# The last unit of a Hymba block: second token block in two halves, given queue orders, fewer sums between products, first block scaled by GpSimd

## The chip, the cores and the metric

The kernel runs on one core of one Trainium2 chip. The metric is device time in microseconds (us), as the median of several runs. TensorE (PE in the profile) multiplies matrices, VectorE (DVE) and ScalarE (ACT) work elementwise, GpSimd (POOL) too, but cannot read the accumulation banks (PSUM); SyncE (SP) issues the DMAs in this kernel. All engines run their own instructions in order and wait for each other through semaphores.

## The reference

One decoder layer on 2048 tokens of width 1024, in float32, cut to its outline:

```python
h = rmsnorm(x, norm1_g)
...                                   # projection, gated linear attention, short convolution
x = x + concatenate([o_gla, o_conv]) @ w_out
h2 = rmsnorm(x, norm2_g)
x = x + (silu(h2 @ w_ffn_gate) * (h2 @ w_ffn_up)) @ w_ffn_down     # 1024 -> 2816 -> 1024
return rmsnorm(x, norm_f_g)           # x * rsqrt(mean(x*x) + 1e-6) * norm_f_g
```

The change concerns the end of this: the last piece of the product with `w_ffn_down`, the residual addition, and the final rmsnorm of the last 1024 tokens.

## The kernel before

Data lie transposed: 128 partitions are 128 of the 1024 features, the free dimension is tokens. There are four blocks of 512 tokens (`PB`), handled as two halves of two blocks. A tile `y[d, j]` holds features 128d to 128d+127 (d from 0 to 7, `KD` = 8) of block j of the half.

Every operand of the big products is split in a high and a low fp32r part, by ACT (`act.activation(hi, src, AF.Copy)`, line 153) and VectorE (the difference, line 154). `product_step` then issues three matmuls per 128 features: high x high (line 381), high x low (382), low x high (383), each on 128x128 weights and 128x512 data. Most products go through `unit`, which computes a 2x2 block of outputs (two feature tiles r, two token blocks j) from seven instead of eight products; sums of weights for it run on GpSimd (lines 364 to 371).

The product with `w_ffn_down` is cut in four groups of inner features (`GROUPS`) and, within a group, in four units of two output tiles (d0 = 0, 2, 4, 6). In the last group of the second half each finished `y` is added up (line 982: on VectorE if the value lies in PSUM or r is not j, else on GpSimd), squared by ACT (lines 790 and 793) and added to `ssq[j]` by GpSimd (line 794), for the final norm.

The last unit of all (d0 = 6) is `last_unit`. It does without the seven-product scheme: four plain products, in the order (r, j) = (0,0), (1,0), (0,1), (1,1), each with 6 steps of 3 matmuls, 18 in all. `tc.issue_after` keeps this order on TensorE. After each product VectorE adds it to `y` (line 1059), ACT squares the result (line 1061), and ACT multiplies `y` by the norm's gain (`gain`, line 1028); the gains of the twelve earlier tiles are multiplied by ACT too, as those become ready. For a block's norm (`norm`) TensorE sums the squares over the partitions by two fp32 matmuls with a matrix of ones (lines 1033 and 1034), ACT takes Ln and Exp (lines 199 and 200), VectorE makes the mean (line 201) and one Newton step of three operations (lines 163 to 165), whose result `rb` lies in PSUM, and ACT copies it to SBUF (line 1036). `scale` then multiplies the eight tiles by `rb`: six on VectorE, two (d = 2 and 5) on GpSimd by the copy (line 1042), and SP stores each, 256 KB, to `out` (line 148).

Within these constraints a list scheduler, which follows a simulated timeline, orders each engine's instructions before the program runs; the order is then fixed. `bank()` takes one of 8 PSUM banks, `tt` and `bt` take SBUF tiles from shared rotating pools; where all are taken, the scheduler makes a new user wait for the release.

Of the kernel before, what the change touches and what calls it, by code (L numbers as in the profile page):

```python
# [14 lines left out]
ALU = mybir.AluOpType  # L15
# [36 lines left out]
def tile_hymba_block(ctx, tc, x, xt, win, wa, wgu, wout, wffn, wdown, wdown_first, small, out):  # L52
# [323 lines left out]
    def product_step(o, w, op, k, first):  # L376
        n = len(op)
        c = slice(k * P, (k + 1) * P)
        wh, wl = w[:, 0, c], w[:, 1, c]
        xh, xl = op[k][:, 0, :], op[k][:, 1, :]  # L380
        pe.matmul(o[:], wh, xh, start=first and k == 0, stop=False, skip_group_check=True)  # L381
        pe.matmul(o[:], wh, xl, start=False, stop=False, skip_group_check=True)  # L382
        return pe.matmul(o[:], wl, xh, start=False, stop=k == n - 1, skip_group_check=True)  # L383
# [634 lines left out]
    def last_unit(src, ops, b12, y, ssq):  # L1018
# [5 lines left out]
        with tc.issue_after(last_hi[0].ins):  # L1024
            act.preload_act_table_set("natural_log_exp_and_others")

        def gain(d, j):
            act.activation(y[d, j], y[d, j], AF.Copy, scale=col(C_GF + d))

        def norm(j, q):  # L1030

            tot, rb = bank("tot"), bank("rb")
            pe.matmul(tot[:], ones[:], ssq[j][:], start=True, stop=False)
            pe.matmul(tot[:], ones[:], q[:], start=False, stop=True)
            finish_rstd(ssq[j], tot, D, rb)
            act.activation(ssq[j][:], rb[:], AF.Copy)
            return rb

        def scale(j, rb):
            for d in range(KD):  # L1040
                eng, by = (pool, ssq[j]) if d in (2, 5) else (dve, rb)
                eng.tensor_tensor(y[d, j], y[d, j], by[:], ALU.mult)
                store(out[2 + j, :, d, :], y[d, j])

        for d in range(KD - 2):
            for j in range(2):
                gain(d, j)
        q, rbs = {}, []
        for j in range(2):
            for r in range(2):  # L1050
                o = bank()
                with ExitStack() as stack:
                    if j or r:
                        stack.enter_context(tc.issue_after(done.ins))
                    for i in range(2):
                        for k in range(len(b12)):
                            done = product_step(o, w[2 * r + i], columns[j][i], k, i == 0)
                yy = y[KD - 2 + r, j]
# [150 lines left out]
```

## Time and profile before

| | us |
|---|---|
| median of 3 runs | 2098.65 |
| the runs | 2098.31, 2098.65, 2102.15 |
| the profiled execution | 2102.39 |
| its span, first to last instruction | 2100.5 |
| mean granted TensorE clock | 0.992 |

The durations and start times in the prediction come from the profiled execution alone, counted from the start of its span. A row of the timeline reads: start, duration, engine, line, operation, output and inputs with their shapes, count; in brackets the idle time of the engine just ahead and the instruction that ended it. A row with a count above 1 merges neighbours. A row of the windows reads: the stretch, its length, busy time and count of PE, PEld (weight loads), DVE, ACT and POOL, then the granted clock of TensorE, the DMA engines' busy share, and GB/s. A row for one line of code reads: operations, minimum, median and maximum duration in ns, first and last start. SPq is SP's issuing of a DMA; the data move later. One fp32 matmul with the ones matrix appears as two records.

### The profile page before, as it was taken

To read this page: it belongs to the slowest core of one execution; us is meant where nothing else is said; L and a number is where in the kernel's file an instruction comes from. 1 tells how busy PE (TensorE), PEld (TensorE's weight loads), DVE (VectorE), ACT (ScalarE), POOL (GpSimd) and SP (SyncE) were. 2 spreads that over 40 slices of the span, in tenths; PEclk is the share of its full clock that TensorE was granted. 3 is DMA by queue.
4 is the path that set the end of the run, shared out by engine and by line. 5 is a ranking of instruction groups with operands and counts; after the bars stand their busy time and mean duration, and the time that the engine had idled before them with its cause. 6 is when DMAs were issued, how large, how long until landed. Compare 5 with 4: busy or idle time off the path is not lost.

```text
span 2100.5 us, 26873 instructions
## 1 busy us (share of the span) xinstructions
PE 2034.6 (97%) x9133; PEld 1649.8 (79%) x9133; DVE 1420.2 (68%) x1983; ACT 1003.2 (48%) x1990; POOL 971.9 (46%) x703
## 2 busy tenths in 40 slices
PE   6999999999999999999999999999999999999996
PEld 4768888877888878788888878787888888877774
DVE  7669786549743786788887665555767766665554
ACT  6555455656542345545545443333545444453344
POOL 3436322222102464465464338774655445436764
PEclk9999999999999999999999999999999999999998
DMA  7359495425686873655646687698444554587673
GB/s 279 129 167 318 128 340 158 149 81 167 205 281 236 325 251 105 236 200 214 223 175 220 236 314 269 234 344 321 159 178 165 192 210 174 213 340 271 259 270 110
DMA packets 189241, 464.43 MB, mean 221 GB/s; under 512 B 19824, under 2 KB 65072, under 8 KB 179504
## 3 DMA queue, kind: packets, MB, share of 16 engines
q1 hardware_dynamic: 189104, 462.72, 61.1%
q8 instruction: 72, 1.18, 0.2%
q14 instruction: 65, 0.53, 0.1%
HBM read 297.49 MB, written 165.15 MB: 220 GB/s over the span
## 4 chain that ended last, share of the span: by engine, by line
PE 74%; DVE 10%; DMA 8%; issue 3%; POOL 3%; ACT 3%; SPq 0%; DVEq 0%; POOLq 0%; ACTq 0%
PE mm L381 22%; PE mm L383 22%; PE mm L382 22%; DVE wq L154 2%; DVE h L508 2%; PE mm L812 1%; DVE op L154 1%; PE mm L813 1%; PE mm L815 1%; DVE so L154 1%; DMA raw<-in_wffn_dram 1%; DMA raw<-in_wdown_dram 1%; DMA op<-shT 1%; PE a_ps L576 1%; DVE c L405 1%
## 5 line engine op out<-in xcount | busy, mean ns | idle before, releaser
L381 PE MATMUL mm<-op,wq 128*128 128x512 f32 x2499 | 981.6, 395 | 17.8 <-ACT wq L153 7.4
L382 PE MATMUL mm<-op,wq 128*128 128x512 f32 x2499 | 976.9, 391 | 0.0
L383 PE MATMUL mm<-op,wq 128*128 128x512 f32 x2499 | 966.4, 392 | 10.4 <-DVE wq L154 9.6
L154 DVE TENSOR_TENSOR wq<-raw,wq 128x512 fp32r<-128x512 f32 (+2 forms) x626 | 527.7, 850 | 333.2 <-ACT wq L153 330.4
L153 ACT ACTIVATE wq<-raw 128x512 fp32r<-128x512 f32 (+2 forms) x626 | 363.5, 587 | 548.6 <-PE mm L383 391.5
L381 PEld LDWEIGHTS mm<-op,wq 128*128 128x128 f32 x2499 | 471.1, 189 | 132.0 <-ACT wq L153 13.5
L383 PEld LDWEIGHTS mm<-op,wq 128*128 128x128 f32 x2499 | 471.1, 189 | 121.2 <-DVE wq L154 22.6
L382 PEld LDWEIGHTS mm<-op,wq 128*128 128x128 f32 x2499 | 471.1, 189 | 97.0 <-issue 1.0
L366 POOL TENSOR_TENSOR raw<-s,raw 128x512 f32<-128x512 f32 (+2 forms) x97 | 127.6, 1316 | 422.6 <-DVE wq L154 402.5
L405 DVE TENSOR_TENSOR c<-mm,c 128x512 f32<-128x512 f32 x267 | 183.0, 685 | 94.4 <-PE mm L383 92.1
L364 POOL TENSOR_TENSOR s<-raw 128x512 f32<-128x512 f32 (+2 forms) x97 | 129.4, 1334 | 205.3 <-DMA raw<-in_wffn_dram 98.7
L371 POOL TENSOR_TENSOR raw<-raw 128x512 f32<-128x512 f32 (+2 forms) x97 | 126.8, 1307 | 129.6 <-DVE wq L154 122.4
L401 ACT ACTIVATE c<-mm 128x512 f32<-128x512 f32 x267 | 155.0, 586 | 39.0 <-PE mm L383 37.7
L794 POOL TENSOR_TENSOR ssx<-ssx,q 128x512 f32<-128x512 f32 x52 | 75.8, 1470 | 158.7 <-ACT q L793 158.5
L365 POOL TENSOR_TENSOR raw<-raw 128x512 f32<-128x512 f32 (+2 forms) x97 | 135.1, 1392 | 4.0
L982 POOL TENSOR_TENSOR y<-c,y 128x512 f32<-128x512 f32 x66 | 98.7, 1497 | 57.3 <-DVE c L405 53.2
L154 DVE TENSOR_TENSOR so<-t,so 128x512 fp32r<-128x512 f32 x100 | 90.7, 913 | 24.4 <-ACT so L153 24.0
L153 ACT ACTIVATE wq<-s 128x512 fp32r<-128x512 f32 (+2 forms) x97 | 56.8, 586 | 98.7 <-PE mm L383 86.0
L812 PE MATMUL mm<-op,wq 128*128 128x512 f32 x256 | 100.9, 395 | 0.0
L813 PE MATMUL mm<-op,wq 128*128 128x512 f32 x256 | 99.8, 390 | 0.0
L154 DVE TENSOR_TENSOR wq<-s,wq 128x512 fp32r<-128x512 f32 (+2 forms) x97 | 84.0, 866 | 17.0 <-ACT wq L153 16.4
L153 ACT ACTIVATE so<-t 128x512 fp32r<-128x512 f32 x100 | 62.5, 626 | 37.8 <-DMA sa_B<-so 16.1
(181 smaller groups left out, 1880.3 us busy)
## 6 DMA issues: line engine op xcount, KB each, us to landing
raw<-in_wffn_dram SPq DMA_DIRECT2D x44, 1024.0 KB, 6.1
sa_T<-so SPq DMA_DIRECT2D x88, 512.0 KB, 4.9
op<-sa_T SPq DMA_DIRECT2D x88, 512.0 KB, 9.4
sa_B<-so SPq DMA_DIRECT2D x69, 512.0 KB, 3.4
op<-sa_B SPq DMA_DIRECT2D x69, 512.0 KB, 9.0
raw<-in_win_dram SPq DMA_DIRECT2D x23, 1024.0 KB, 5.4
raw<-in_wdown_dram SPq DMA_DIRECT2D x24, 768.0 KB, 6.1
sx<-y SPq DMA_DIRECT2D x48, 256.0 KB, 3.3
```

The source lines that it names most:

```text
L153: last_hi[:] = [act.activation(hi, src, AF.Copy)]
L154: return dve.tensor_tensor(lo, src, hi.bitcast(F32), ALU.subtract)
L364: pool.tensor_tensor(s1, a21, a22, ALU.add)
L365: pool.tensor_tensor(a21, a11, a21, ALU.subtract)
L366: pool.tensor_tensor(a11, s1, a11, ALU.subtract)
L371: pool.tensor_tensor(a12, a12, a11, ALU.subtract)
L381: pe.matmul(o[:], wh, xh, start=first and k == 0, stop=False, skip_group_check=True)
L382: pe.matmul(o[:], wh, xl, start=False, stop=False, skip_group_check=True)
L383: return pe.matmul(o[:], wl, xh, start=False, stop=k == n - 1, skip_group_check=True)
L401: act.activation(t[:], o[:], AF.Copy)
L405: dve.tensor_tensor(t[:], o[:], t[:], ALU.add)
L812: pe.matmul(o[e, j][:], wh, m[:, 0, :], start=k == 0, stop=False)
```

## The change

Block 0 is still handled whole; block 1 is handled in two halves of 256 columns (tokens), `sa` and `sb`, through products, squares, sums, factor, scaling and stores. `queued` gives TensorE and VectorE one written-out order each for everything in the unit that goes through it. The sums use a matrix of 1/1024 (`means`) and Newton's step is rewritten, so that line 201's operation falls away and a constant -0.5 moves into the gains. Block 0's gains stay on ACT, for tiles 0 to 6; its tiles 0 to 6 are scaled by GpSimd, tile 7 by VectorE with gain and factor in one operation. All of block 1 is scaled by VectorE in that form, gain included; ACT multiplies no gains for block 1. The stores of block 1 are 16 of 128 KB instead of 8 of 256 KB.

```diff
@@ -373,14 +373,14 @@
         w["A22"] = weight_quarter(a22)
         return w
 
-    def product_step(o, w, op, k, first):
+    def product_step(o, w, op, k, first, s=slice(0, PB)):
         n = len(op)
         c = slice(k * P, (k + 1) * P)
         wh, wl = w[:, 0, c], w[:, 1, c]
-        xh, xl = op[k][:, 0, :], op[k][:, 1, :]
-        pe.matmul(o[:], wh, xh, start=first and k == 0, stop=False, skip_group_check=True)
-        pe.matmul(o[:], wh, xl, start=False, stop=False, skip_group_check=True)
-        return pe.matmul(o[:], wl, xh, start=False, stop=k == n - 1, skip_group_check=True)
+        xh, xl = op[k][:, 0, s], op[k][:, 1, s]
+        pe.matmul(o[:, s], wh, xh, start=first and k == 0, stop=False, skip_group_check=True)
+        pe.matmul(o[:, s], wh, xl, start=False, stop=False, skip_group_check=True)
+        return pe.matmul(o[:, s], wl, xh, start=False, stop=k == n - 1, skip_group_check=True)
 
     def unit(src, ops, into=None):
 
@@ -1023,50 +1023,124 @@
         columns = (ops["B11"], ops["B21"]), (b12, ops["B22"])
         with tc.issue_after(last_hi[0].ins):
             act.preload_act_table_set("natural_log_exp_and_others")
-
-        def gain(d, j):
-            act.activation(y[d, j], y[d, j], AF.Copy, scale=col(C_GF + d))
-
-        def norm(j, q):
-
-            tot, rb = bank("tot"), bank("rb")
-            pe.matmul(tot[:], ones[:], ssq[j][:], start=True, stop=False)
-            pe.matmul(tot[:], ones[:], q[:], start=False, stop=True)
-            finish_rstd(ssq[j], tot, D, rb)
-            act.activation(ssq[j][:], rb[:], AF.Copy)
+        known = bt("known", (P, P + KD))
+        means, gains = known[:, 0:P], known[:, P : P + KD]
+        dve.memset(means, 1.0 / D)
+        dve.tensor_scalar(gains, sml[:, C_GF : C_GF + KD], -0.5, None, ALU.mult)
+        halves = slice(0, PB // 2), slice(PB // 2, PB)
+        whole = slice(0, PB)
+        queues = {}
+
+        def queued(eng, issue):
+            with ExitStack() as stack:
+                if eng in queues:
+                    stack.enter_context(tc.issue_after(queues[eng].ins))
+                queues[eng] = issue()
+
+        def steps(o, r, j, s):
+            for i in range(2):
+                for k in range(len(b12)):
+                    queued(pe, lambda: product_step(o, w[2 * r + i], columns[j][i], k, i == 0, s))
+                    yield
+
+        def product(r, j, s):
+            o = bank()
+            for _ in steps(o, r, j, s):
+                pass
+            return o
+
+        def residual(o, r, j, s):
+            yy = y[KD - 2 + r, j][:, s]
+            queued(dve, lambda: dve.tensor_tensor(yy, o[:, s], yy, ALU.add))
+            q = tt("q")
+            act.activation(q[:, s], yy, AF.Square)
+            return q
+
+        def summed(tot, q, s, first=False, last=False):
+            queued(pe, lambda: pe.matmul(tot[:, s], means, q[:, s], start=first, stop=last))
+
+        def logs(j, tot, s):
+            l, y0 = bt("l"), bt("y0")
+            act.activation(l[:, s], tot[:, s], AF.Ln, bias=eps[:])
+            act.activation(y0[:, s], l[:, s], AF.Exp, scale=-0.5)
+            return l, y0
+
+        def factor(j, tot, s, l, y0):
+
+            rb = bank("rb")
+            queued(dve, lambda: dve.tensor_tensor(l[:, s], y0[:, s], y0[:, s], ALU.mult))
+            queued(
+                dve,
+                lambda: dve.scalar_tensor_tensor(
+                    l[:, s], tot[:, s], EPS, l[:, s], ALU.add, ALU.mult
+                ),
+            )
+            queued(
+                dve,
+                lambda: dve.scalar_tensor_tensor(
+                    rb[:, s], l[:, s], -3.0, y0[:, s], ALU.add, ALU.mult
+                ),
+            )
             return rb
 
-        def scale(j, rb):
-            for d in range(KD):
-                eng, by = (pool, ssq[j]) if d in (2, 5) else (dve, rb)
-                eng.tensor_tensor(y[d, j], y[d, j], by[:], ALU.mult)
-                store(out[2 + j, :, d, :], y[d, j])
+        def scale(ds, j, s, rb):
+            for d in ds:
+                yy, g = y[d, j][:, s], gains[:, d : d + 1]
+                queued(
+                    dve,
+                    lambda: dve.scalar_tensor_tensor(yy, yy, g, rb[:, s], ALU.mult, ALU.mult),
+                )
+                store(out[2 + j, :, d, s], yy)
+
+        def scale_beside(ds, j, s):
+            for d in ds:
+                yy = y[d, j][:, s]
+                pool.tensor_tensor(yy, yy, ssq[j][:, s], ALU.mult)
+                store(out[2 + j, :, d, s], yy)
 
         for d in range(KD - 2):
-            for j in range(2):
-                gain(d, j)
-        q, rbs = {}, []
-        for j in range(2):
-            for r in range(2):
-                o = bank()
-                with ExitStack() as stack:
-                    if j or r:
-                        stack.enter_context(tc.issue_after(done.ins))
-                    for i in range(2):
-                        for k in range(len(b12)):
-                            done = product_step(o, w[2 * r + i], columns[j][i], k, i == 0)
-                yy = y[KD - 2 + r, j]
-                dve.tensor_tensor(yy, o[:], yy, ALU.add)
-                q[j] = tt("q")
-                act.activation(q[j][:], yy, AF.Square)
-                gain(KD - 2 + r, j)
-                if not r:
-                    pool.tensor_tensor(ssq[j][:], ssq[j][:], q[j][:], ALU.add)
-                if j and not r:
-                    rbs.append(norm(0, q[0]))
-        rbs.append(norm(1, q[1]))
-        for j in range(2):
-            scale(j, rbs[j])
+            act.activation(y[d, 0], y[d, 0], AF.Copy, scale=gains[:, d : d + 1])
+
+        sa, sb = halves
+        tot = [bank("tot") for _ in range(3)]
+        o = product(0, 0, whole)
+        q = residual(o, 0, 0, whole)
+        act.activation(y[KD - 2, 0], y[KD - 2, 0], AF.Copy, scale=gains[:, KD - 2 : KD - 1])
+        pool.tensor_tensor(ssq[0][:], ssq[0][:], q[:], ALU.add)
+        o = product(1, 0, whole)
+        q7 = residual(o, 1, 0, whole)
+        o = product(0, 1, sa)
+        p = residual(o, 0, 1, sa)
+        pool.tensor_tensor(ssq[1][:, sa], ssq[1][:, sa], p[:, sa], ALU.add)
+        summed(tot[0], ssq[0], whole, first=True)
+        o = bank()
+        for n, _ in enumerate(steps(o, 1, 1, sa)):
+            if n == 2:
+                summed(tot[0], q7, whole, last=True)
+        l0 = logs(0, tot[0], whole)
+        p7 = residual(o, 1, 1, sa)
+        o = product(0, 1, sb)
+        summed(tot[1], ssq[1], sa, first=True)
+        rb0 = factor(0, tot[0], whole, *l0)
+        act.activation(ssq[0][:], rb0[:], AF.Copy)
+        scale_beside(range(KD - 1), 0, whole)
+        scale((KD - 1,), 0, whole, rb0)
+        r = residual(o, 0, 1, sb)
+        o = bank()
+        for n, _ in enumerate(steps(o, 1, 1, sb)):
+            if n == 0:
+                summed(tot[1], p7, sa, last=True)
+        l1 = logs(1, tot[1], sa)
+        summed(tot[2], ssq[1], sb, first=True)
+        summed(tot[2], r, sb)
+        rb1 = factor(1, tot[1], sa, *l1)
+        scale((0, 1), 1, sa, rb1)
+        r7 = residual(o, 1, 1, sb)
+        summed(tot[2], r7, sb, last=True)
+        l2 = logs(1, tot[2], sb)
+        scale((2, 3, 4, 5, 6, 7), 1, sa, rb1)
+        rb2 = factor(1, tot[2], sb, *l2)
+        scale(range(KD), 1, sb, rb2)
 
 
     act.preload_act_table_set("natural_log_exp_and_others")
```

## The prediction

> **What bounds the kernel now.** I read the share of the engines first, then the chain that ended last, then the timeline of the last 65 us engine by engine, then the windows of clock and DMA.
>
> ```profile
> PE 2034.6 (97%) x9133; PEld 1649.8 (79%) x9133; DVE 1420.2 (68%) x1983; ACT 1003.2 (48%) x1990; POOL 971.9 (46%) x703
> 2070.32 0.39 PE L381 MATMUL mm<-op,wq 128*128 128x512 f32 x1
> 2070.81 1.29 POOL L1064 TENSOR_TENSOR ssx<-ssx,q 128x512 f32<-128x512 f32 x1
> 2074.40 1.02 PE L1033 MATMUL tot<-ssx,ones 128*128 128x512 f32 x2
> 2075.26 1.02 PE L1034 MATMUL tot<-q,ones 128*128 128x512 f32 x2
> 2080.24 1.02 PE L1033 MATMUL tot<-ssx,ones 128*128 128x512 f32 x2
> 2080.80 3.68 DVE L1042 TENSOR_TENSOR y<-y,rb 128x512 f32<-128x512 f32 x6 [0.66 <-ACT ssx L1036]
> 2084.40 0.69 DVE L1059 TENSOR_TENSOR y<-mm,y 128x512 f32<-128x512 f32 x1
> 2085.80 2.07 PE L1034 MATMUL tot<-q,ones 128*128 128x512 f32 x2 [4.54 <-ACT q L1061]
> 2087.91 0.69 ACT L199 ACTIVATE l<-tot,eps 128x512 f32<-128x512 f32 x1 [1.41 <-PE tot L1034]
> 2088.63 0.63 ACT L200 ACTIVATE y<-l 128x512 f32<-128x512 f32 x1
> 2090.74 0.70 DVE L165 SCALAR_TENSOR_TENSOR rb<-l,y 128x512 f32<-128x512 f32 x1
> 2091.47 0.60 ACT L1036 ACTIVATE ssx<-rb 128x512 f32<-128x512 f32 x1 [2.22 <-DVE rb L165]
> 2092.10 3.68 DVE L1042 TENSOR_TENSOR y<-y,rb 128x512 f32<-128x512 f32 x6 [0.66 <-ACT ssx L1036]
> 2092.82 4.46 SPq L148 DMA_DIRECT2D out_dram<-y  x8
> 2093.50:2093.75 0.25, 0.00 (x0) 0.00 (x0) 0.25 (x1) 0.00 (x0) 0.25 (x1) 0.50 0.38 147
> 2098.00:2099.00 1.00, 0.00 (x0) 0.00 (x0) 0.00 (x0) 0.00 (x0) 0.00 (x0) 0.50 1.00 389
> 2099.20:2099.40 0.20, 0.00 (x0) 0.00 (x0) 0.00 (x0) 0.00 (x0) 0.00 (x0) 0.50 0.04 10
> ```
>
> TensorE is busy for 97% of the span, but the change lies behind its last products. Those end where the sums for block 1 begin, at 2080.24. From there to 2100.5 nothing is bound by products. The addition for the last product (L1059) starts only at 2084.40, because six scalings of block 0 hold VectorE from 2080.80: some 4 us. The sum behind it finds TensorE idle for 4.54 us and takes 2.07 us. Then come Ln, Exp, three VectorE steps, a copy, and scaling from 2092.10. All 2 MB of block 1 leave after that: the first bytes move at about 2093.65, 0.83 us behind their issue at 2092.82, and at 389 GB/s they last until 2099.2. The span ends 1.3 us later.
>
> **The products in halves.** The first product of block 1 starts at 2070.32 and its 18 matmuls take 4.08 us, 0.227 each. The change makes 36 such matmuls into 72 with 256 columns. No row shows that form; the nearest is the mixer's fp32 matmul, where a record loads 128 columns and streams 128 columns twice, 256 in all (the ones-matmul's two records for 512 columns take 0.86 us, four passes):
>
> ```profile
> 329.23 0.38 PE L736 MATMUL o_ps<-vt,scores 128*128 128x128 f32 x2
> 330.79 0.39 PE L738 MATMUL o_ps<-carry,kq 128*128 128x128 f32 x2
> L736 PEld LDWEIGHTS o_ps<-vt,scores x128: 187/192/192, 290.1 to 648.4; 128*128 128x128 f32 x128
> ```
>
> Fourteen records lie between these two starts: 0.111 each. The weight load's 0.19 us is thus overlapped, and I take 0.113, half of 0.227. The ends are 0.111 and the 0.227 of today. The sums: from 2074.40 to 2075.26 one ones-matmul takes 0.86, so half a one 0.43. TensorE's line from 2070.32: 18 halves (2.03), the first sum of block 0 (0.86), 9 halves (1.02), its second sum (0.86), to 2075.09; 9 and 18 halves, to 2078.14; half a sum, three halves, half a sum (1.20), to 2079.34; 15 halves, to 2081.04; two half sums, to 2081.9. The last product is issued 0.8 later than today's, since two whole and two half sums stand between the products where two whole ones did. One place is tight: GpSimd's addition to block 0's squares ends at 2072.1 (2070.81 + 1.29), and TensorE now asks for it at 2072.35; were it later, every half product would wait behind that sum.
>
> **VectorE and GpSimd.** The durations:
>
> ```profile
> L508 DVE SCALAR_TENSOR_TENSOR h<-h,sml,rb_ps x48: 732/736/749, 14.9 to 1068.5; 128x512 f32<-128x512 f32 x48
> L702 DVE SCALAR_TENSOR_TENSOR kq<-kq,ee x16: 410/425/1518, 212.8 to 627.1; 128x256 f32<-128x256 f32 x16
> L1042 POOL TENSOR_TENSOR y<-y,ssx 128x512 f32<-128x512 f32 x4 | 5.0, 1268 | 12.3 <-ACT ssx L1036 12.3
> 1206.38 0.42 DVE L154 TENSOR_TENSOR wq<-raw,wq 128x256 fp32r<-128x256 f32 x1
> 1207.58 2.98 DVE L154 TENSOR_TENSOR wq<-raw,wq 128x256 fp32r<-128x256 f32 x2 [0.18 <-ACT wq L153]
> 1207.54 1.30 POOL L915 TENSOR_TENSOR t<-c,t 128x512 f32<-128x512 f32 x1 [1.49 <-DVE c L911]
> 1208.80 1.48 POOL L915 TENSOR_TENSOR t<-c,c 128x512 f32<-128x512 f32 x1
> L699 ACT ACTIVATE ee<-ee 128x256 f32<-128x256 f32 x16 | 6.6, 413 | 18.4 <-DMA ee<-sd 16.9 <-DMA vt<-sv 1.5
> ```
>
> The new scaling is the form of L508 (data, a column of gains, a factor in PSUM), 0.736 whole. Half of it I take as 0.47, less 0.27 as between whole and half tensor_tensor (0.69 and 0.42), and 0.40 back to back, since six of today's take 3.68. Operations with both inputs in SBUF are another matter: L702 takes 0.41 or 1.52, and the pair at 1207.58, 0.42 each alone, takes 2.98 with GpSimd operations at 1207.54 and 1208.80: each waits for one of GpSimd's to end, and GpSimd's next is 0.18 longer. In the new factor the square of y0 and the last step read SBUF twice; the middle one reads PSUM.
>
> VectorE's line: Block 0's sum is readable at 2075.3, Ln and Exp (0.69, 0.63) end at 2076.65. The half addition for the (1,1) half, 2076.35 to 2076.77; factor of block 0, 3 x 0.70, to 2078.9. ACT copies the factor (0.60) and GpSimd starts seven multiplications at 2079.5, 1.27 each. One scaling (0.70), one half addition (0.42), to 2080.0. Block 1a's Ln and Exp (0.45 each, from L699's 0.41 for an activation) end at 2080.45. Its factor costs 3 x 0.38 = 1.14 alone; beside GpSimd I add half an operation's wait before the first step and what is left of the next after the middle step, 1.15 in all: to 2082.75. Two half scalings (0.84) and the last addition (0.42), to 2083.97: it starts 0.85 ahead of today's, and only half the width is left. Behind it queue six half scalings (2.4), to 2086.4. They hide the last square (0.42), half sum (0.43, 0.2 to drain), Ln and Exp, which end at 2085.9. Were that cover gone, its 1.9 would count. The second factor, beside GpSimd, 2.0, to 2088.4; eight half scalings, 3.2, to 2091.6. GpSimd ends at 2079.5 + 8.9 + four insertions of 0.33, about 2089.7; its last store isn't late.
>
> **Stores.** Sixteen stores become 24 on SP's one queue.
>
> ```profile
> 208.79 1.85 SPq L145 DMA_DIRECT2D vt<-sv  x4
> 210.69 1.85 SPq L145 DMA_DIRECT2D gt<-sg  x4
> ```
>
> Eight small ones start every 0.475 us (1.90 between groups of four); the eight of 256 KB above took 4.46, 0.56 each, at the rate the data moves (0.68). A 128 KB store needs 0.34 at 389 GB/s, so SP's issue is the limit. The last eight start at 2088.9, and I put two of GpSimd's among them (its sixth ends at 2088.1): nine gaps of 0.475, so the last issue is at 2093.2, past VectorE's 2091.6. Add 0.83 to first bytes, 0.34 to move, 1.3 to the end: 2095.7, against 2100.5: **4.8 less**. Rows of 1 KB instead of 2 have no row here; the data would have to fall to 276 GB/s (128 KB in 0.475) before they count. The bounds: SP keeps up with VectorE, 6.4 less; SP at 0.56, and so 1.0 behind from the twelve stores since 2083.2, 3.1 less. Half matmuls of 0.227 give 1.3 less (rival 2).
>
> Against the move to GpSimd speaks the page GPSIMD Engine Reference of the Trainium skill (Engine selection), which sends elementwise work with two inputs to VectorE, as about twice slower on GpSimd. The trace agrees on the ratio, 1.27 against the 0.69 of a whole tensor_tensor. Done by that rule, seven operations of 0.69 would stand in VectorE's line, which sets the end here, and the sum would be 4.8 worse; by the rows the line goes without them, and GpSimd's 10.2 fit beside it.
>
> **Ahead of the unit.** Today's gains run on ACT for both blocks; the change keeps block 0's alone, and seven of them. A memset and a column of gains are new on VectorE, small and early; it idles for 32% of the span.
>
> ```profile
> 2033.17 0.63 ACT L793 ACTIVATE q<-y 128x512 f32<-128x512 f32 x1 [1.78 <-DVE y L982]
> 2033.84 0.72 ACT L1028 ACTIVATE y<-y,sml 128x512 f32<-128x512 f32 x1
> 2034.47 0.92 ACT L153 ACTIVATE wq<-raw 128x384 fp32r<-128x384 f32 x2
> 2036.21 0.63 ACT L793 ACTIVATE q<-y 128x512 f32<-128x512 f32 x1 [0.83 <-DVE y L982]
> 2037.38 0.62 PE L381 MATMUL mm<-op,wq 128*128 128x512 f32 x1 [2.59 <-ACT c L401]
> 2038.66 0.63 PE L381 MATMUL mm<-op,wq 128*128 128x512 f32 x1
> 2039.94 0.63 PE L381 MATMUL mm<-op,wq 128*128 128x512 f32 x1
> 2049.73 1.32 ACT L1028 ACTIVATE y<-y,sml 128x512 f32<-128x512 f32 x2
> 2053.87 0.50 PE L381 MATMUL mm<-op,wq 128*128 128x512 f32 x1 [0.33 <-ACT c L401]
> ```
>
> The gain at 2033.84 follows the square of a DVE-added value of block 1 (row not equal to column in the unit) and stands ahead of a weight split; TensorE then idles 2.59 us, waiting for ACT, and runs nine matmuls at 0.43 (three in 1.28). The gain gone, 0.6 of the idle goes; the pair at 2049.73 likewise takes the 0.33 at 2053.87. I count 1.0 less. The bounds: 2.8 less, if the shorter idle keeps the clock up (nine times 0.2), and nothing; beyond nothing, a rival below.
>
> **Sum.** 4.8 + 1.0 = 5.8 less. The profiled execution took 2102.39, its span 2100.5 and 1.9 around it; it would take 2096.6. It lies 3.7 above the median of the runs, 2098.65, one of which took 2102.15; I take the difference off the median: 2092.9.
>
> **Rivals.** A measurement here can tell about 0.2%, 4.2 us, from no change.
>
> (1) *The lock and SP's queue eat it.* If each of the four double-SBUF steps waits for a whole GpSimd operation (L702: 1.52 instead of 0.43, 1.1 each, 4.4 where I count 2.1), or SP's stores wait in order behind GpSimd's, the tail saves 2.5 and the whole about 3.5: 2095.2, within 0.2%. For it, seven GpSimd operations back to back; against it, the pair at 1207.58, where VectorE got in between. The page SBUF — State Buffer of the Trainium skill (Who interferes with whom) says that the later one is blocked fully, which is this rival.
>
> (2) *Half-width matmuls that aren't half.* Slower: if 256 columns went at the pace of the fp32 ones-matmul, 0.43 each, the products would end at 2103.9 (2070.32, 72 x 0.43, 1.72 and 0.86 of sums); then addition, square and half sum with their drains 1.7, Ln and Exp 0.9, factor 1.14, the first scaling 0.47, seven store gaps 3.3 and 2.5 of tail, 10.0 in all: 2113.9, 13.4 more, a time of 2112.0. Decided by the pitch: at 0.227 the products end at 2089.2 and the span at 2099.2; slower begins above 0.24, and by 0.2% above 0.30. Against it, 0.111 at 329 to 331.
>
> (3) *ACT's order ahead of the unit.* With eight gains gone the instructions are interleaved anew, and a copy may stand behind a later square as at 2036.21. One new stall of the size at 2037.38 costs 2.6 + 1.8 = 4.4: 2097.3, no change; two of them, 2101.7.
>
> (4) *The order isn't kept:* if the last addition still followed all of block 1a's scalings, 2.4 would return: 2095.3; it is put into VectorE's order, so I give it nothing.
>
> **How the numbers follow.** Forecast 0.68, 2089.5 to 2094.4 (both best bounds at the low end); rival 1: 0.15; rival 2: 0.07, of which 0.06 slower; rival 3: 0.10, of which 0.06 slower. So faster 0.68, same 0.15 + 0.01 + 0.04 = 0.20, slower 0.12. The range, 2089.5 to 2098.9, takes in rival 1 and one stall of rival 3 and leaves out the slower cases and a little at the low end.
>
> **What would show it.** Right: matmuls of 128x256 starting every 0.11 to 0.12; the last addition at about 2084 less what is saved ahead; GpSimd busy for about 10 us without a gap; SP's last eight stores every 0.48; TensorE's idle at 2037 shorter. Wrong: a pitch near 0.2; the factor's steps at 1.5 each; TensorE idling ahead of 2066 where it doesn't now; the last store over 3 us behind the last scaling.

## The result and the profile after

| | us |
|---|---|
| before, median of 22 runs | 2102.96 |
| after, median of 22 runs | 2098.03 |
| ratio after / before | 0.9974, 95% interval 0.9967 to 0.998 |
| the profiled execution after | 2099.24 |
| its span | 2097.2 |
| mean granted TensorE clock | 0.993 |

The change makes the kernel faster by 0.26%, 4.9 us between the medians (5.5 by the ratio, 4.2 to 6.9 by its interval). Both medians lie higher than the 2098.65 that was shown before; the ratio, taken side by side, is what counts.

Single executions of this kernel drift against each other by several microseconds long before the last unit. Therefore I read the end of every trace from a mark of its own: the start of the first matmul of block 1 in `last_unit`. From it to the end of the span I call the *tail*: 30.18 us before (2100.5 less 2070.32) and 25.56 after (2097.2 less 2071.64), 4.62 less.

The shares of the engines on the page after:

```profile
PE 2034.3 (97%) x9175; PEld 1652.7 (79%) x9175; DVE 1415.2 (67%) x1993; ACT 997.8 (48%) x1984; POOL 975.4 (47%) x706
```

Nothing is to be learnt there: TensorE's 97% hides a change of 4.6 us. The timeline of the end, after, engine by engine:

```profile
2071.64 0.28 PE L381 MATMUL mm<-op,wq 128*128 128x256 f32 x1
2073.67 0.28 PE L383 MATMUL mm<-op,wq 128*128 128x256 f32 x1
2082.81 0.59 PE L1060 MATMUL tot<-ssx,known 128*128 128x256 f32 x2
2085.85 0.70 PE L1060 MATMUL tot<-q,known 128*128 128x256 f32 x2 [2.01 <-ACT q L1056]
2082.18 0.49 DVE L1071 TENSOR_TENSOR l<-y 128x256 f32<-128x256 f32 x1
2083.16 0.94 DVE L1080 SCALAR_TENSOR_TENSOR rb<-l,y 128x256 f32<-128x256 f32 x1
2084.93 0.42 DVE L1054 TENSOR_TENSOR y<-mm,y 128x256 f32<-128x256 f32 x1
2085.26 2.43 DVE L1091 SCALAR_TENSOR_TENSOR y<-y,known,rb 128x256 f32<-128x256 f32 x6
2087.61 0.42 DVE L1071 TENSOR_TENSOR l<-y 128x256 f32<-128x256 f32 x1
2088.52 0.92 DVE L1080 SCALAR_TENSOR_TENSOR rb<-l,y 128x256 f32<-128x256 f32 x1
2089.47 3.22 DVE L1091 SCALAR_TENSOR_TENSOR y<-y,known,rb 128x256 f32<-128x256 f32 x8
2081.10 9.46 POOL L1098 TENSOR_TENSOR y<-y,ssx 128x512 f32<-128x512 f32 x7 [5.42 <-ACT ssx L1125]
2081.83 13.05 SPq L148 DMA_DIRECT2D out_dram<-y  x24
2092.02 1.89 SPq L148 DMA_DIRECT2D out_dram<-y  x4
2094.00 0.88 SPq L148 DMA_DIRECT2D out_dram<-y  x2
```

The last addition (L1054, 2084.93) no longer stands behind block 0's scalings: counted from the mark it starts at 13.3 instead of 14.1, with half the width left, and the six scalings behind it cover the last square, sum, Ln and Exp: VectorE stands idle for no longer than 0.04 at a time between 2081.06 and 2092.69. The last scaling ends 21.05 after the mark instead of 25.46, 4.41 less; the stores, now 24, end 4.62 less. What the data did, in the windows of the same trace (the last number of a row is GB/s):

```profile
2083.00:2084.00 1.00, 0.84 (x4) 0.38 (x3) 0.97 (x2) 0.00 (x0) 1.00 (x2) 1.00 1.02 385
2088.00:2089.00 1.00, 0.00 (x0) 0.00 (x0) 0.93 (x3) 0.00 (x0) 1.00 (x1) 0.50 1.00 362
2094.00:2095.00 1.00, 0.00 (x0) 0.00 (x0) 0.00 (x0) 0.00 (x0) 0.00 (x0) 0.50 0.78 265
```

With 256 KB stores alone the DMA engines are full at 385. At 2088 they are full at 362, with 128 KB stores (rows of 1 KB) of block 1 and 256 KB stores of GpSimd's tiles side by side; what the small ones reach alone is seen in e4. At the very end they are not full: 265 GB/s is one 128 KB store every 0.49 us, the pace at which SP issues them (four from 2092.02 to 2094.00).

### The profile page after: what moved, and what is told of

It is laid out like the page before. It is cut to its first block, busy times and chain, and to the rows that moved or that the text cites. A ratio compares the mean times of both kernels' runs of the same rounds, so it can differ in the third digit from the quotient of the medians.

```text
span 2097.2 us, 26987 instructions
## 1 busy us (share of the span) xinstructions
PE 2034.3 (97%) x9175; PEld 1652.7 (79%) x9175; DVE 1415.2 (67%) x1993; ACT 997.8 (48%) x1984; POOL 975.4 (47%) x706
## 4 chain that ended last, share of the span: by engine, by line
PE 76%; DVE 9%; DMA 7%; issue 3%; POOL 2%; ACT 2%; SPq 0%; DVEq 0%; ACTq 0%; POOLq 0%
PE mm L381 23%; PE mm L383 23%; PE mm L382 22%; DVE wq L154 2%; DVE h L508 2%; PE mm L812 1%; PE mm L813 1%; PE mm L815 1%; DVE so L154 1%; DVE op L154 1%; DMA raw<-in_wdown_dram 1%; DMA op<-shT 1%; DMA raw<-in_wffn_dram 1%; PE a_ps L576 1%; DVE c L405 1%
## 5 line engine op out<-in xcount | busy, mean ns | idle before, releaser
L154 DVE TENSOR_TENSOR wq<-raw,wq 128x512 fp32r<-128x512 f32 (+2 forms) x626 | 525.0, 846 | 334.2 <-ACT wq L153 332.1
L401 ACT ACTIVATE c<-mm 128x512 f32<-128x512 f32 x267 | 155.0, 586 | 38.7 <-PE mm L383 37.5
L794 POOL TENSOR_TENSOR ssx<-ssx,q 128x512 f32<-128x512 f32 x52 | 75.8, 1469 | 158.7 <-ACT q L793 158.5
L982 POOL TENSOR_TENSOR y<-c,y 128x512 f32<-128x512 f32 x66 | 99.0, 1502 | 58.0 <-DVE c L405 58.0
L154 DVE TENSOR_TENSOR so<-t,so 128x512 fp32r<-128x512 f32 x100 | 90.2, 906 | 24.9 <-ACT so L153 24.6
L154 DVE TENSOR_TENSOR wq<-s,wq 128x512 fp32r<-128x512 f32 (+2 forms) x97 | 83.9, 865 | 17.0 <-ACT wq L153 16.5
```

Source lines behind the costliest of these rows:

```text
L154: return dve.tensor_tensor(lo, src, hi.bitcast(F32), ALU.subtract)
L401: act.activation(t[:], o[:], AF.Copy)
```

## The experiments

The theory (A): nearly all of the gain comes from one thing, that VectorE adds the last product before it scales block 0, not after. Its rivals: it needs the halves (B), or it needs GpSimd's share of the scalings (C). For what is left behind it the end may be set by SP's issue (S), by the data rate (D), or by VectorE's line (V). Into this line counts what I call the lock: a VectorE step with two inputs in SBUF waits while a GpSimd operation runs; e5 tests it. In the table, all times but the ratio are from the profiled execution; the end of the last scaling and the tail are counted from the mark.

| kernel | mark | span | last scaling ends | tail | tail less before | ratio to before, 95% interval |
|---|---|---|---|---|---|---|
| before | 2070.32 | 2100.5 | 25.46 | 30.18 | | |
| after | 2071.64 | 2097.2 | 21.05 | 25.56 | -4.62 | 0.9974 (0.9967 to 0.998) |
| e1, before with the order alone | 2067.57 | 2093.7 | 21.39 | 26.13 | -4.05 | 0.9979 (0.9969 to 0.999) |
| e2, after without halves | 2074.99 | 2102.7 | 22.88 | 27.71 | -2.47 | 0.9986 (0.9975 to 0.9997) |
| e3, after, VectorE scales block 0 | 2074.25 | 2101.2 | 23.61 | 26.95 | -3.23 | 0.9981 (0.9968 to 0.9994) |
| e4, after, two issuing queues | 2069.28 | 2094.4 | 21.04 | 25.12 | -5.06 | 0.9973 (0.9963 to 0.9983) |
| e5, after without the lock | 2064.48 | 2089.4 | 19.78 | 24.92 | -5.26 | 0.9970 (0.9957 to 0.9983) |
| e6, after, early sums | 2073.20 | 2101.4 | 21.22 | 28.20 | -1.98 | 0.9987 (0.9975 to 0.9998) |
| e7, e4 + e5 + early sums | 2072.61 | 2096.9 | 19.81 | 24.29 | -5.89 | 0.9967 (0.9955 to 0.9979) |
| e8, before with the gains moved | 2067.74 | 2097.7 | 26.81 | 29.96 | -0.22 | one run |
| e9, e6 with the stores sorted | 2068.29 | 2093.5 | 21.21 | 25.21 | -4.97 | 0.9973 (0.9964 to 0.9983) |
| e10, e4 + e5 | 2066.68 | 2091.1 | 19.78 | 24.42 | -5.76 | 0.9973 (0.9962 to 0.9983) |

The ratios of the variants overlap; only against before do they stand alone. The comparisons among variants therefore rest on the tails, each from one execution. Of the computing in them, pairs in which it is the same show how well it repeats: the last scaling ends at 21.22 and 21.21 in e6 and e9, at 19.78 in e5 and in e10. How well the stores behind it repeat was not measured.

**e1: the order alone.** The kernel before, with one wait: block 0's scalings come after the last addition.

```diff
-                eng.tensor_tensor(y[d, j], y[d, j], by[:], ALU.mult)
+                with tc.issue_after(added.ins):
+                    eng.tensor_tensor(y[d, j], y[d, j], by[:], ALU.mult)
...
-                dve.tensor_tensor(yy, o[:], yy, ALU.add)
+                added = dve.tensor_tensor(yy, o[:], yy, ALU.add)
```

> The kernel before, with one thing of the change: the last product's addition stands ahead of block 0's six scalings in VectorE's order. The measure in the trace is the tail, from the first matmul of block 1's first product to the end of the span: 30.18 us before (2070.32 to 2100.5), 25.56 after (2071.64 to 2097.2). Theory A (most of the change's gain is that the last addition no longer waits for the scalings): addition at 2080.4 to 2081.1, square to 2081.8, sum on a warm TensorE to 2082.9, Ln and Exp to 2084.2; the six scalings fill VectorE to 2084.8, factor to 2087.6, copy wait 0.7, first store 0.7 later at 2089.0 instead of 2092.8: tail 26.3, 3.8 shorter, about 0.18% of the time. Rival B (the halves make the gain): the six scalings then stand ahead of the second factor instead and the 2 MB still leave at once: tail 29 or more.

The timeline of e1, and a row of its windows:

```profile
2077.69 0.69 DVE L1060 TENSOR_TENSOR y<-mm,y 128x512 f32<-128x512 f32 x1 [0.31 <-PE mm L383]
2078.29 3.67 DVE L1043 TENSOR_TENSOR y<-y,rb 128x512 f32<-128x512 f32 x6
2079.09 1.12 PE L1034 MATMUL tot<-q,ones 128*128 128x512 f32 x2 [0.59 <-ACT q L1062]
2085.28 3.68 DVE L1043 TENSOR_TENSOR y<-y,rb 128x512 f32<-128x512 f32 x6 [0.66 <-ACT ssx L1036]
2090.00:2091.00 1.00, 0.00 (x0) 0.00 (x0) 0.00 (x0) 0.00 (x0) 0.00 (x0) 0.50 1.03 385
```

VectorE waits 0.31 us for the last product and adds it; the six scalings start 0.24 later than before, counted from the mark (10.72 against 10.48), because before they had to wait 0.66 for ScalarE's copy anyway. In return the sum's idle time falls from 4.54 to 0.59 and the sum itself from 2.07 to 1.12. The tail is 4.05 shorter, 26.13 where A expected 26.3: one line of order gives most of what the whole change gives. Its end is set by data at 385 GB/s in full-size stores (the windows row).

**e2: the change without halves.** Block 1 goes whole through products, sums, factor and scaling; the order, GpSimd's seven scalings and the gains in the scaling stay. Both sums of block 0 stand right behind block 1's first product.

```diff
-        o = product(0, 1, sa)
-        p = residual(o, 0, 1, sa)
+        o = product(0, 1, whole)
+        p = residual(o, 0, 1, whole)
...
-        scale((2, 3, 4, 5, 6, 7), 1, sa, rb1)
-        rb2 = factor(1, tot[2], sb, *l2)
-        scale(range(KD), 1, sb, rb2)
+        scale(range(KD), 1, whole, rb1)
```

> The changed kernel with block 1 in one piece of 512 columns: given orders, GpSimd's seven scalings and the folded gains stay; both sums of block 0 come right behind block 1's first product. Theory A: the order and GpSimd carry the gain; last addition at about 2080.5 (on the time axis of before), factor beside GpSimd to 2087.5, eight scalings of 0.67, stores from 2088.2 at the data's 0.68 each with two of GpSimd's among them: tail 26.9, 3.3 shorter than before and 1.3 longer than after. Rival B (halves carry it): tail 29 or more.

Timeline and windows of e2:

```profile
2085.93 0.69 DVE L1054 TENSOR_TENSOR y<-mm,y 128x512 f32<-128x512 f32 x1
2089.87 0.93 DVE L1071 TENSOR_TENSOR l<-y 128x512 f32<-128x512 f32 x1 [3.26 <-ACT y L1065]
2085.31 9.52 POOL L1098 TENSOR_TENSOR y<-y,ssx 128x512 f32<-128x512 f32 x7 [3.31 <-ACT ssx L1119]
2090.00:2091.00 1.00, 0.00 (x0) 0.00 (x0) 0.96 (x2) 0.00 (x0) 1.00 (x2) 1.00 0.57 219
2098.00:2099.00 1.00, 0.00 (x0) 0.00 (x0) 0.00 (x0) 0.00 (x0) 0.00 (x0) 0.50 1.00 379
```

27.71, between the two expectations and 1.6 worse than the order alone. GpSimd yields one 256 KB tile in 1.36 us (9.52 over seven), 193 GB/s, and in the meantime VectorE has nothing to scale: it idles 3.26 us for the square, the sum, Ln and Exp. So the DMA engines run at 219 while they could do 380, and the rest is stored afterwards at 379. Without the halves, moving block 0 to GpSimd costs; that is read from these rows, since e2 and e1 also differ in the factor's steps and in the gains.

**e3: VectorE scales block 0.** The change with six of block 0's tiles on VectorE and two on GpSimd, as before.

```diff
-        scale_beside(range(KD - 1), 0, whole)
-        scale((KD - 1,), 0, whole, rb0)
+        scale_beside((2, 5), 0, whole)
+        scale((0, 1, 3, 4, 6, 7), 0, whole, rb0)
```

> The changed kernel with block 0 scaled as before the change: tiles 2 and 5 on GpSimd, six on VectorE, these with the gain folded in. Theory A (the end is set by the stores: in the trace after, the last one is issued 1.8 us behind VectorE's last scaling): VectorE's line grows by five whole scalings, 3.3, and loses up to 1.0 of waiting for GpSimd, so its end moves by 2.3 and the stores' by about 0.6 only: tail 26.2. Rival C (GpSimd's scaling is what gains): the whole 3.3 shows: tail 28.9.

The timeline of e3, with two rows of TensorE, and two rows of its windows:

```profile
2088.54 0.70 PE L1060 MATMUL tot<-q,known 128*128 128x256 f32 x2 [2.52 <-ACT q L1056]
2091.03 1.22 PE L1060 MATMUL tot<-q,known 128*128 128x256 f32 x2 [1.80 <-ACT q L1056]
2083.66 4.04 DVE L1091 SCALAR_TENSOR_TENSOR y<-y,known,rb 128x512 f32<-128x512 f32 x6 [0.72 <-ACT ssx L1124]
2088.86 0.43 DVE L1080 SCALAR_TENSOR_TENSOR rb<-l,y 128x256 f32<-128x256 f32 x1
2090.12 0.42 DVE L1054 TENSOR_TENSOR y<-mm,y 128x256 f32<-128x256 f32 x1
2094.64 3.22 DVE L1091 SCALAR_TENSOR_TENSOR y<-y,known,rb 128x256 f32<-128x256 f32 x8
2088.50:2089.50 1.00, 0.70 (x2) 0.30 (x2) 0.93 (x3) 0.00 (x0) 0.00 (x0) 1.00 1.03 383
2090.50:2091.50 1.00, 0.47 (x1) 0.47 (x2) 1.00 (x4) 0.42 (x1) 0.00 (x0) 0.52 0.94 339
```

26.95, nearer to A's 26.2 than to C's 28.9. The factor's last step is 0.43 beside an idle GpSimd instead of 0.94, but the six scalings stand ahead of the second half's additions again: the last addition starts 15.87 after the mark (2090.12) instead of 13.29, and the last scaling ends 2.56 later than after. Only 1.39 of it reaches the end, because the stores have less to catch up: the tail behind the last scaling falls from 4.51 to 3.34. The halves without GpSimd are, in this order, worth less than the order alone on whole blocks (-3.23 against -4.05). But e3 takes away GpSimd's share and the early place of the last addition at once: halves with block 0's scalings on VectorE behind the last addition were not tried. What is shown is that halves and GpSimd together give 0.57 over e1, and neither of them as e2 and e3 have it does.

**e4: a second issuing queue.** Every other store of the last half is issued by ScalarE, which has nothing else to do by then.

```diff
-                store(out[2 + j, :, d, s], yy)
+                if other and d % 2:
+                    act.dma_start(out[2 + j, :, d, s], yy)
+                else:
+                    store(out[2 + j, :, d, s], yy)
```

> The changed kernel with every other store of the last half issued by ACT, which is idle by then; nothing else differs. Theory S (SP's issue, 0.475 to 0.5 a store, sets the end): VectorE's last scaling sets it instead, and the end comes about 1.8 earlier: tail 23.8. Rival D (the data set it: the DMA engines are at 0.95 to 1.0 from 2087 to 2092.5, and 1.15 MB are left at 2092.0, 3.1 us at 366 GB/s): 0.7 earlier: tail 24.9.

Timeline and windows of e4:

```profile
2088.01 2.69 ACTq L1094 DMA_DIRECT2D out_dram<-y  x4
2091.00:2092.00 1.00, 0.00 (x0) 0.00 (x0) 0.00 (x0) 0.00 (x0) 0.00 (x0) 0.50 0.98 337
```

25.12: D's 24.9 is nearly met, S's 23.8 is not. The issue limit is gone (337 GB/s at a DMA share of 0.98 instead of 265 at 0.78), yet only 0.44 us of the tail goes with it: the data had a backlog, and in 128 KB stores alone, as in this row, the DMA engines are as good as full at 337, not at 385. The Trainium skill, DMA: Bandwidth & Descriptors (Issuing engines are not separate DMA queues), says that a second issuing engine saves the issue time alone, since the same 16 DMA engines do the work. The run agrees; that the issue time is usually small beside the transfer doesn't hold for this store, 0.49 against 0.39 (128 KB at 337 GB/s).

**e5: no lock.** Exp writes its result in the factor's PSUM bank and ScalarE squares it, so no VectorE step of the factor reads SBUF twice, and VectorE has two steps instead of three.

```diff
-            l, y0 = bt("l"), bt("y0")
+            l, y0 = bt("l"), bank("rb")
...
+            act.activation(l[:, s], y0[:, s], AF.Square)
...
-            rb = bank("rb")
-            queued(dve, lambda: dve.tensor_tensor(l[:, s], y0[:, s], y0[:, s], ALU.mult))
+            rb = y0
```

> The changed kernel with the factor rebuilt so that no step of it has two inputs in SBUF: Exp is written to the factor's own PSUM bank, ACT squares it (one more ACT operation a factor), and VectorE has two steps instead of three. Tail after: 25.56 (first matmul of block 1's first product to the end of the span). The factors of the two halves take 1.92 and 1.83 there, with the last step at 0.93. Expected: last steps at 0.43 to 0.47, VectorE's last scaling 1.0 earlier. Theory D (since e4: the data of the stores set the end, near full rate from five us behind the first store): the tail shortens by 0.4 at most, to 25.2. Rival V (VectorE's line sets the end): all of the 1.0 shows, 24.6.

The timeline of e5:

```profile
2080.12 0.42 DVE L1074 SCALAR_TENSOR_TENSOR l<-tot,l 128x256 f32<-128x256 f32 x1 [0.24 <-ACT l L1066]
2080.58 0.43 DVE L1080 SCALAR_TENSOR_TENSOR rb<-l,rb 128x256 f32<-128x256 f32 x1
2073.79 8.68 POOL L1098 TENSOR_TENSOR y<-y,ssx 128x512 f32<-128x512 f32 x7 [5.28 <-ACT ssx L1125]
```

24.92, in the middle between D (25.2) and V (24.6). The last step falls from 0.92 to 0.43, and GpSimd's operation from 1.35 to 1.24 in the mean: the lock cost both sides. The last scaling ends 1.27 earlier, not by the lock alone, since e5 also takes a VectorE step out of each factor. Of this, 0.64 arrives at the end; the rest waits behind the data and SP.

**e6: earlier sums.** Both sums of block 0 right behind the first half product, and its factor ahead of the addition of the second.

```diff
-        for n, _ in enumerate(steps(o, 1, 1, sa)):
-            if n == 2:
-                summed(tot[0], q7, whole, last=True)
+        summed(tot[0], q7, whole, last=True)
         l0 = logs(0, tot[0], whole)
...
+        o = product(1, 1, sa)
+        p7 = residual(o, 1, 1, sa)
         scale((KD - 1,), 0, whole, rb0)
```

> The changed kernel with both sums of block 0 right behind the first half product of block 1, and block 0's factor ahead of the (1,1) half's addition in VectorE's order; nothing else differs. Block 0's factor and so GpSimd's first multiplication and the first store come about 1.1 earlier. Theory D (the data set the end): about 0.2 MB more have left by the time the engines are saturated, 0.5 less: tail 25.0. Rival V (VectorE's line or SP's issue behind the second factor sets the end): these start no earlier, tail 25.5.

28.20: both theories were wrong, and by much. SP's waits, and windows, of e6:

```profile
SPq L148 <- POOL y L1098: 34.8, 7, 29.7
2091.00:2092.00 1.00, 0.00 (x0) 0.00 (x0) 0.96 (x4) 0.00 (x0) 0.00 (x0) 0.50 0.27 100
2095.00:2096.00 1.00, 0.00 (x0) 0.00 (x0) 0.00 (x0) 0.00 (x0) 0.00 (x0) 0.50 0.79 268
```

Computing ends at 21.22, almost as after (21.05), but the DMA engines stand at 100 GB/s while finished tiles of block 1 lie about, and then from 2094 to 2100 they are fed at SP's pace, 263 to 269. SP waited for GpSimd seven times, 5.1 us beside the 29.7 before the first store: the scheduler's simulated timeline had put all eight stores of block 0 ahead of the sixteen of block 1, so every ready half waited behind GpSimd's last tile. e9 tries this reading.

**e9: e6 with the stores sorted.** SP's order written out by the time the tiles became ready in e6. The order of all other engines' instructions is that of e6.

```diff
+        turn = [(0, d, 0) for d in (7, 0, 1, 2)]
+        turn += [(1, 0, 0), (1, 1, 0), (0, 3, 0), (1, 2, 0), (1, 3, 0), (0, 4, 0)]
...
+        for key in turn:
+            queued(nc.sync, lambda: store(*ready[key]))
```

> The kernel with both sums of block 0 right behind the first half product, and SyncE's 24 output stores written in the order in which that run's tiles became ready: block 0's row 7, rows 0 to 2, then block 1's first-half rows between GpSimd's rows 3 to 6, and the second half's last; before, all eight stores of block 0 stood ahead of all of block 1's. Every other engine's instructions and their order are unchanged, so the last scaling should end 21.2 us behind the first matmul of block 1 as it did. Theory H (ready stores were held behind a store that waited for GpSimd): the tail falls from 28.2 to 25.4 us (25.0 to 25.9), level with the changed kernel's 25.6. Theory M (what made that run long is not the order of the stores, but that the data moves slower or GpSimd's own end comes later): the tail stays at 27.5 us or more.

SP's waits in e9:

```profile
SPq L148 <- POOL y L1100: 2.0, 3, 1.0
```

25.21 as H expected (25.4), 2.99 less than e6 with the last scaling at the same place. The order of the stores alone was the 3 us.

**e7 and e10: the gains together.** e7 is e4, e5 and e6's early sums in one; the scheduler happened to interleave its stores (SP waits for GpSimd 2.5 us in all). e10 is e4 and e5 without the early sums.

> The changed kernel with the early sums, the factor without two SBUF inputs, and every other store of the last half issued by ACT. Theory D: the data start 1.1 earlier, the stretches in which the DMA engines now idle fill, and the last ones leave as VectorE ends: tail 24.0, 1.5 shorter than after; against the kernel before 6.2 less, ratio 0.997. Rival: the parts don't add, because 4.2 MB at 370 GB/s need 11.3 us behind the first store anyway: 24.7.

> The changed kernel with both the first estimate squared by ScalarE in a PSUM bank (two VectorE steps for a factor instead of three) and every other store of the last half issued by ScalarE's queue; the sums of block 0 stay where the change has them. Theory N (the early sums of the kernel with all three edits brought nothing; its gain is that of the other two): the last scaling ends 19.8 us behind the first matmul of block 1, the tail is 24.3 us (24.1 to 24.6). Theory E (the early sums carried part of it, because the data starts to flow earlier): 24.7 us or more, that is no better than the 24.92 of the run without the lock by more than a quarter of a microsecond.

The last scalings end at 19.81 and 19.78 and the tails are 24.29 and 24.42: on top of the other two edits the early sums bring 0.13, N is right. Alone, with the stores sorted as well (e9), the tail is 0.35 shorter than after. With 0.9967 (0.9955 to 0.9979) e7 has the best ratio seen, against 0.9974 of the change; the intervals overlap, so that it beats the change is likely by its tail (1.27 shorter) and not shown by its times.

**e8: the gains alone.** The kernel before without ScalarE's gains for block 1; VectorE scales all eight tiles of block 1, by gain and factor at once. Only the stretch ahead of the unit is read.

```diff
         for d in range(KD - 2):
-            for j in range(2):
-                gain(d, j)
+            gain(d, 0)
...
-                gain(KD - 2 + r, j)
+                if j == 0:
+                    gain(KD - 2 + r, j)
```

> The kernel before without ACT's gains for block 1; VectorE multiplies them in as it scales block 1, all eight tiles. Only the stretch ahead of the last unit is read: the idle of TensorE at 2037.38 (2.59) and 2053.87 (0.33) of before. The prediction: 2.0 and none. Rival L (as the trace after suggests: the split's difference on VectorE starts 0.6 earlier, meets GpSimd's addition of squares and takes 1.33 instead of 0.57, so nothing is left): 2.59 and about none.

The stall ahead of the unit, in the timelines of before, of after and of e8:

```profile
2033.88 1.28 POOL L794 TENSOR_TENSOR ssx<-ssx,q 128x512 f32<-128x512 f32 x1 [1.76 <-ACT q L793]
2035.01 0.57 DVE L154 TENSOR_TENSOR wq<-raw,wq 128x384 fp32r<-128x384 f32 x1 [1.87 <-ACT wq L153]
```

```profile
2035.57 1.29 POOL L794 TENSOR_TENSOR ssx<-ssx,q 128x512 f32<-128x512 f32 x1 [1.76 <-ACT q L793]
2035.94 1.33 DVE L154 TENSOR_TENSOR wq<-raw,wq 128x384 fp32r<-128x384 f32 x1 [1.11 <-ACT wq L153]
2037.20 0.68 DVE L982 TENSOR_TENSOR y<-mm,y 128x512 f32<-128x512 f32 x1
2037.91 0.63 ACT L793 ACTIVATE q<-y 128x512 f32<-128x512 f32 x1 [0.87 <-DVE y L982]
2038.44 1.07 ACT L401 ACTIVATE c<-mm 128x512 f32<-128x512 f32 x2
2039.08 0.50 PE L381 MATMUL mm<-op,wq 128*128 128x512 f32 x1 [2.59 <-ACT c L401]
2055.18 0.50 PE L381 MATMUL mm<-op,wq 128*128 128x512 f32 x1
```

```profile
2031.59 1.28 POOL L794 TENSOR_TENSOR ssx<-ssx,q 128x512 f32<-128x512 f32 x1 [1.77 <-ACT q L793]
2031.95 1.33 DVE L154 TENSOR_TENSOR wq<-raw,wq 128x384 fp32r<-128x384 f32 x1 [1.11 <-ACT wq L153]
2035.08 0.69 PE L381 MATMUL mm<-op,wq 128*128 128x512 f32 x1 [2.59 <-ACT c L401]
```

The idle time is 2.59 in all three: L's number, not the prediction's 2.0. With the gain gone, the split's difference on VectorE (L154) starts 0.76 us sooner after GpSimd's start, and yet ends where it did, 0.41 to 0.42 after GpSimd's end (2035.16 and 2035.58 before, 2036.86 and 2037.27 after, 2032.87 and 2033.28 in e8). The middle fence shows the rest of the chain: behind that difference comes VectorE's addition (L982), behind it its square on ScalarE, and behind the square, in ScalarE's order, the copies that TensorE waits for. So the stall hangs on GpSimd's L794, and the gain stood in its shadow. That it is the lock that holds the difference is read from these ends; the kernel with L794 elsewhere was not tried.

The second gap, at 2053.87 before, shrinks in e8 as well, but not by the gains alone. From the start of one matmul to the next it is 0.71 before and 0.28 after (2054.90 to 2055.18). In e1, whose instructions up to there are those of before, it is 0.45 (2050.65 to 2051.11), and in e8, without the gains, 0.43 (2050.85 to 2051.28).

## Why the prediction was right, and which step was not

Predicted were 5.8 us less. The traces account for 4.6 in the tail and for 0.1 to 0.4 ahead of it; the medians are 4.9 apart, and the times alone, with 4.2 to 6.9, can't tell 5.8 from 4.9. As a time, 2098.03 lies outside the 2089.5 to 2094.4 of the forecast proper and inside the range only where it had been kept for rivals 1 and 3. That is the base and not the mechanism: the 2092.9 started from the 2098.65 of three runs; from the 2102.96 beside which the change was measured, the same 5.8 leads to 2097.2. That the time still falls inside the range, by 0.9, is luck. The steps of the tail, with after's times less 1.32 (the two marks, 2071.64 and 2070.32) beside the prediction's:

| step | predicted | measured |
|---|---|---|
| pitch of a half matmul | 0.113 | 0.119 (2071.64 to 2073.67, 17 gaps) |
| GpSimd starts seven scalings | 2079.5 | 2079.78 |
| first half's factor done | 2082.75 | 2082.78 |
| last addition starts | 2083.55 | 2083.61 |
| second half's factor done | 2088.4 | 2088.12 |
| GpSimd done | 2089.7 | 2089.24 |
| last scaling ends | 2091.6 | 2091.37 |
| SP's last stores, start to start | 0.475 | 0.49 |
| last store issued | 2093.2 | 2093.2 |
| span ends | 2095.7 | 2095.88 |

- **The tail, 4.8 predicted, 4.6 measured.** The line of steps holds to 0.5 at every point. Its credit was spread wrongly in one respect: I wrote the halves and GpSimd as parts of the sum, but e1 has 4.05 of it from the order alone, and e2 and e3, each with one of the other two, have less than that. The price of 4.8 for seven GpSimd operations done by VectorE was too high: e3, with five more there, lengthens VectorE's line by 2.56 and the tail by 1.39.
- **The lock.** Counted at two waits in each factor. Measured, the first step hardly waits (0.49, 0.42), only the last does (0.94, 0.92, against 0.43 in e5 and, beside an idle GpSimd, in e3), half a microsecond each time; GpSimd's operations take 1.35 in the mean instead of 1.24. Where a step stands against GpSimd's operations decides: the last steps start in the middle of one and end 0.3 behind its end (2084.10 behind 2082.36 + 1.46, 2089.44 behind 2087.63 + 1.52), the first ones happen to start shortly ahead of an end. The first factor ended where predicted because two misses cancel: it starts 0.41 later than I had it (2080.86 against 2080.45) and takes 1.92 instead of 2.30. The second takes 1.83 instead of 2.0.
- **SP's issue as the limit.** Right for the last store: from 2086.06 to 2094.00 SP issues sixteen stores, one every 0.50, and the last at the time predicted. But it was not the only limit. e4 takes it away and gets 0.44, because the DMA engines were nearly full too, at shares of 0.99 to 1.03 from 2087 to 2092. The rate of small rows, for which I had no row, is 337 GB/s (e4), still above the 276 below which I meant it to count; what I left out is that GpSimd's 256 KB stores, one every 1.35 us, stand among the small ones. At one issue every 0.50 this asks for some 360 GB/s, an estimate from these figures, as much as the engines move there.
- **The clock.** The last sum finds TensorE idle for 2.01 us, and its two records take 0.70, against 0.59 for the sum at 2082.81: nearly at full speed, for the granted clock is still 1.00 (0.98 over 2087 to 2088). Covered, it costs nothing.
- **The term that failed: 1.0 ahead of the unit.** For the pair of gains 0.33 was counted. The gap behind it is 0.43 shorter after than before, but in e1, which keeps the gains, it is 0.26 shorter too. From the end of the stall to the mark the traces with the gains take 32.94 (before) and 32.73 (e1), those without 32.66 (e8) and 32.56 (after): what the pair brought lies between 0.1 and 0.4, and more can't be said from single executions. The 0.6 from the stall at 2037 didn't come; it is 2.59 as before, because the bound was GpSimd's operation, not the gain in ScalarE's line. I had read the releaser (ScalarE's L401) and the nearest instruction that goes, and had not asked what the instruction behind it would meet.
- **The rivals.** (1) needed a wait for a whole GpSimd operation, 1.52 in all, for every double-SBUF step: out by 0.94. But its second half, SP's in-order queue holding stores behind GpSimd's, is real; the change escapes it (two waits, 1.2 in all), e6 does not and loses 2.6. (2) is out by the pitch of 0.119. (3): no new stall at 2037 or 2055. (4): the order was kept.

The Trainium skill, SBUF — State Buffer (Who interferes with whom), has the port pair of VectorE and GpSimd as an exclusive lock and nothing else as shared. e5 agrees: with no step of the factor that reads SBUF twice, the stretched 0.92 is 0.43.

## What to carry to other kernels

Before splitting work or moving it to another engine, look at which instruction stands ahead of the one that a whole chain waits for; one line of order gave here what the large change gave, less 0.6. A fixed queue of stores is part of that order: when producers on two engines finish at different paces, write the stores out by the time the tiles become ready, or the DMA engines starve behind the slow one. And before counting on an instruction that is taken off an engine, look at what its successor will meet: here it met a GpSimd operation, and the wait stayed as long.

## What was not expected of the hardware

- A 128 KB store of 128 rows of 1 KB occupies SP's issuing for 0.49 us, more than its data need (0.39 at 337 GB/s); a stream of such stores from one queue runs at 263 to 269 GB/s (e6), from two at 337 (e4).
- VectorE's 256-column step with two SBUF inputs took 0.92 to 0.94 when it started in the middle of a GpSimd operation, 0.42 to 0.49 when one was about to end, 0.43 alone; the GpSimd operations rose from 1.24 to 1.35 in the mean.
- The length of TensorE's last wait doesn't tell whether the sum behind it runs slow: in e3 the sum after 2.52 us of idle time took 0.70, and the next, after only 1.80, took 1.22. The granted clock does tell: it is 1.00 in the windows row of the first and 0.52 in that of the second.
- The same idle time need not have the same effect. Behind the 2.59 us of the stall the granted clock falls to 0.50 for about 3 us before (2038 to 2041), but in e5, where the stall is 2.59 too, every window from 2033 to 2038 has 1.00, and from the stall's end to the mark it takes 31.32 us instead of 32.94 before and 32.56 after. The code of e5 differs from after's in the factor alone, so this looks like a part of the drift between executions. What decides it was not tried.
